# A list scheduler's model of VectorE and GpSimd: mutual exclusion in place of a share, and ScalarE's table loads counted

## The chip, the cores and the metric

The kernel runs on one core of a Trainium2 chip, as one program. The metric is device time in microseconds (us): the median of several executions. Engines are called by their names: TensorE (PE in the profile, its weight loads PEld), VectorE (DVE), ScalarE (ACT), GpSimd (POOL) and SyncE (SP). SP and GpSimd also issue the transfers (DMAs) of this kernel.

## The reference

The kernel computes a small encoder in float32: one batch of 512 tokens with 1024 features, two layers. Each layer has four sub-steps, and every one adds its result to the input and normalises:

```python
for i in range(DEPTH):
    y = swiglu(x, ffn_w_gate[i, 0], ffn_w_up[i, 0], ffn_w_down[i, 0])
    x = layer_norm(ALPHA * x + 0.5 * y, ln_g[i, 0], ln_b[i, 0])
    y = mixer_ab(...) if i % 2 == 0 else mixer_c(...)
    x = layer_norm(ALPHA * x + y, ln_g[i, 1], ln_b[i, 1])
    y = memory_attn(x, mem, mem_w_q[i], mem_w_kv[i], mem_w_o[i])
    x = layer_norm(ALPHA * x + y, ln_g[i, 2], ln_b[i, 2])
    y = swiglu(x, ffn_w_gate[i, 1], ffn_w_up[i, 1], ffn_w_down[i, 1])
    x = layer_norm(ALPHA * x + 0.5 * y, ln_g[i, 3], ln_b[i, 3])
```

`swiglu` is silu(x W_gate) * (x W_up) W_down with 2816 hidden features. `mixer_ab` has eight dense attention heads (A, with RMS-normed queries and keys) and eight heads in a window of 128 tokens to either side with a sink (B); both get rotary positions. `mixer_c` is a neighbourhood attention of 16 heads on an 8 by 64 grid with a learned bias. `memory_attn` attends to 256 memory tokens with four heads.

## The kernel before

**Tiling and stages.** Every float32 operand of a matmul is split into a high and a low part (`split`): ScalarE rounds it to the fast float32 format, VectorE subtracts the rounded value from the original, and a product is three matmuls (`mm3`). The split subtractions, 128 partitions by 1024 or 512 columns, are the bulk of VectorE's work. The eight stages run one after the other with some overlap: feed-forward, mixer AB, memory attention, feed-forward, feed-forward, mixer C, memory attention, feed-forward. The feed-forward parts save multiplications with seven products for eight (`quarters`, `down_steps`), whose sums VectorE makes, in part with DMAs that add (issued by GpSimd).

**What GpSimd computes.** It multiplies softmax weights by the reciprocal of their sums (`normalise`, form t<-t,l; some go to VectorE as a tensor_scalar), adds the two halves of the rotary embedding (`rope`, form slab<-t,t), subtracts the bias from the mask in mixer C (t<-near,t), adds collected sums to the rows (`gather`, form x<-x,slab), and takes the reciprocal square roots of the norms (`rsqrt`, tiles lny, rms2y, rms8y). Beside that it issues DMAs. In the feed-forward parts it does hardly anything but issue DMAs; in the mixers it computes all the time.

**The scheduler.** The kernel isn't issued as it is written. A `Graph` records every instruction of every engine as an `Op` with an estimate of its duration (`cost`, lines 113 to 134; for VectorE 72 ns and columns/0.96, halved columns for a tensor_scalar in SBUF, 60 ns for each per-row scalar; for GpSimd 2.4 ns a column and 70 ns when both operands are dense, else 1.7 and 130), its dependencies and the tiles it holds. `emit` (from line 290) then calls `plan` twice. `plan` (from line 175) is a simulation of a list schedule: for each engine it keeps the operations whose operands have landed, takes the engine that can start first, gives it the operation of the smallest key, and sets its stop and the time its result lands. Tiles come free in the plan when their last user has landed, and go to waiting tiles in the order of the program. In the first pass the key is the place in the program. Between the passes `deadlines` works out for every operation the latest start, back from TensorE's due times. In the second pass that is the key for VectorE, ScalarE and GpSimd; TensorE and SyncE keep the program's order among what is ready. The order in which the second plan starts the operations is the order in which they are issued, engine by engine. On the chip each engine follows its list in order and waits on semaphores for real results. So the plan's times decide orders alone: an operation that the plan thinks early can sit at the head of its engine's list and wait.

**What the plan knew of VectorE and GpSimd together.** `record` marks an operation as `plain` if it is a tensor_tensor without a PSUM operand. When a plain operation of VectorE is planned, 35% of the time that it overlaps with the last four plain operations of GpSimd is added to it. GpSimd's own operations are never made longer, and no other kind of operation is. Loads of ScalarE's function table aren't planned at all.

**Names in the profile.** All instructions recorded have one line, L150 (`op.call`), so groups are told apart by tile: slab, raw and t are tiles in SBUF; a, d and t as the output of a matmul are PSUM banks (t takes mostly transposes; t also names SBUF tiles of 512 columns); x are the rows, xh and xl their split transposes.

Of the kernel before, what the change touches and what calls it, by code (L numbers as in the profile page):

```python
# [16 lines left out]
AF = mybir.ActivationFunctionType  # L17
# [22 lines left out]

class Op:
    __slots__ = (
        "engine", "adds", "ns", "call", "deps", "users", "wait", "ready", "end", "frees", "index", "rank", "dma", "size", "plain",
        "key", "start", "stop", "lands", "later",
    )

# [19 lines left out]
class Graph:  # L66
# [69 lines left out]
    def record(self, engine, method, args, kw):  # L136
        kw = dict(kw)
        aps = [z for z in list(args) + list(kw.values()) if hasattr(z, "tensor")]
        outs = [kw[k] for k in ("out", "accum_out") if k in kw]
        if "out" not in kw:  # L140
            outs.insert(0, args[0])
        ins = [z for z in aps if not any(z is o for o in outs)]
        op = Op()
        op.engine, op.index, op.dma, op.adds = engine, len(self.ops), method == "dma_start", "accum_op" in kw
        op.rank = op.index
        op.ns = self.cost(engine, method, outs[0], ins, kw)
        op.size = math.prod(outs[0].shape) * 4
        op.plain = method == "tensor_tensor" and all(z.space != bass.MemoryType.PSUM for z in ins + outs)
        fn = getattr(getattr(self.nc, engine), method)
        op.call = lambda: fn(*args, **kw)  # L150
        op.deps, op.users, op.frees, op.later = set(), [], [], []
        if self.after and engine in self.after[1]:
            op.deps.add(self.after[0])
        for z, writes in [(z, False) for z in ins] + [(z, True) for z in outs]:
            info = self.tiles.get(z.tensor.name)
            if info is None:
                continue
            p0, p1, runs = self.extent(z)
            opens = writes and kw.get("start", False)
            keep = []  # L160
            for q, w, a0, a1, other in info["log"]:
                over = opens or p0 < a1 and a0 < p1 and (
                    info["bank"] and q.engine != engine or any(l < b and a < h for l, h in runs for a, b in other)
                )
                if over and (w or writes or info["bank"] and q.engine != engine) and q is not op:
                    op.deps.add(q)
                covered = writes and p0 <= a0 and a1 <= p1 and all(any(l <= a and b <= h for l, h in runs) for a, b in other)
                if not covered:
                    keep.append((q, w, a0, a1, other))
            keep.append((op, writes, p0, p1, runs))  # L170
            info["log"] = keep
            info["users"].add(op)
        self.ops.append(op)

    def plan(self):

        for info in self.tiles.values():
            info["left"], info["at"], info["behind"] = len(info["users"]), 0.0, None
        now = {e: 0.0 for e in self.ENGINES}
        heaps = {e: [] for e in self.ENGINES}  # L180
        ready = {e: [] for e in self.ENGINES}
        free = {s: [(0.0, i, None) for i in range(s.bufs)] for s in self.spaces.values()}
        turn = {s: 0 for s in free}
        queues = {True: [(0.0, 0.0)], False: [(0.0, 0.0)]}
        busy, order = [], []
        for op in self.ops:
            op.wait, op.ready = len(op.deps) + len(op.frees), 0.0

        def release(op, t):
            op.ready = max(op.ready, t)  # L190
            op.wait -= 1
            if op.wait == 0:
                heapq.heappush(heaps[op.engine], (op.ready, op.key, op.index, op))

        def grant(space):

            while turn[space] < len(space.queue) and free[space]:
                info = space.queue[turn[space]]
                turn[space] += 1
                if info["users"]:  # L200
                    t, _, info["behind"] = heapq.heappop(free[space])
                    for op in info["users"]:
                        release(op, t)

        def arrive(e):
            while heaps[e] and heaps[e][0][0] <= now[e]:
                _, key, i, op = heapq.heappop(heaps[e])
                heapq.heappush(ready[e], (key, i, op))

        for op in self.ops:  # L210
            if op.wait == 0:
                heapq.heappush(heaps[op.engine], (0.0, op.key, op.index, op))
        for space in free:
            grant(space)
        while len(order) < len(self.ops):
            best = None
            for e in self.ENGINES:
                arrive(e)
                if ready[e] and e in self.PATIENT:
                    key, _, op = ready[e][0]  # L220
                    for at, k, _, _ in heapq.nsmallest(4, heaps[e]):
                        if at < now[e] + op.ns * 0.6 and k < key - self.margin:
                            now[e] = at
                            arrive(e)
                            break
                if ready[e]:
                    t = now[e]
                elif heaps[e]:
                    t = heaps[e][0][0]
                else:  # L230
                    continue
                if best is None or t < best[0]:
                    best = (t, e)
            assert best, "no instruction can start"
            t, e = best
            if not ready[e]:
                now[e] = t
                continue
            _, _, op = heapq.heappop(ready[e])
            shared = lambda pairs, a, b: sum(max(0.0, min(b, y) - max(a, x)) for x, y in pairs)  # L240
            stop = t + op.ns
            if op.plain and e == "vector":
                stop += 0.35 * shared(busy[-4:], t, stop)
            elif op.plain and e == "gpsimd":
                busy.append((t, stop))
            lands = stop + self.LATENCY[e]
            if op.dma:
                kind = e == "sync"
                work = op.size / 2**19 * (4000.0 if op.adds else 1650.0)
                begin = max(stop + (1200.0 if kind else 2000.0), queues[kind][-1][1])  # L250
                finish = begin + work + 0.5 * shared(queues[not kind][-6:], begin, begin + work)
                queues[kind].append((begin, finish))
                lands = finish + 790.0
            op.start, op.stop, op.lands, now[e] = t, stop, lands, stop
            order.append(op)
            for u in op.users:
                release(u, stop if e == u.engine == "tensor" else lands)
            for info in op.frees:
                info["left"] -= 1
                info["at"] = max(info["at"], lands)  # L260
                if info["left"] == 0:
                    heapq.heappush(free[info["space"]], (info["at"], len(order), info))
                    grant(info["space"])
        return order
# [1364 lines left out]
```

## Time and profile before

| what | us |
|---|---|
| median of 3 runs | 2147.38 (2145.44 to 2148.2) |
| the profiled execution's own time | 2146.44 |
| its span, first to last instruction | 2144.3 |
| TensorE busy | 2117.4 |
| VectorE busy | 1761.6 |
| ScalarE busy | 1082.3 |
| GpSimd busy | 377.2 |

The span is what the trace sees of the profiled execution; that execution's own time is 2.1 us more. Groups in the profile read: line, engine, operation, output<-inputs, shape, count, then busy time in all, mean duration of one in ns, and idle time of the engine just before them with what ended it. In views of waits the columns after the names are the total, how often, and the longest. In the windows view each engine's busy time is followed by its number of instructions in brackets, and after GpSimd come the granted clock of TensorE, the busy share of the DMA engines and GB/s. TensorE's matmuls overlap and their ends are modelled, so its busy time is not proof of full speed. The timeline's rows are start, length, engine, operation and count, with idle time before it in square brackets.

The stages in this trace, by the tiles that they touch: feed-forward to about 315 us, mixer AB to 580, memory attention to 770, two feed-forward parts to 1400, mixer C to 1620, memory attention to 1840, feed-forward to 2115, and the last norms and stores to 2144.

### The profile page before, as it was taken

What the parts mean: (1) busy time and instruction counts of PE and PEld (TensorE: products, weight loads), DVE (VectorE), ACT (ScalarE), POOL (GpSimd) and SP (SyncE); (2) the same over time, 40 slices, a digit from 0 to 9 for tenths busy, and PEclk for the clock granted to TensorE, in tenths of its full rate; (3) what the DMA queues carried; (4) which work ended last, traced back from release to release, by engine and by line L of the source; (5) the groups of instructions that cost most, each with busy time, mean ns of one, the idle gap of its engine ahead of it and who ended that gap; (6) DMA issues with size and microseconds to landing.
All of it is one profiled execution on the core that took longest, in us unless ns stands there. A gap on an engine that the chain in (4) does not pass through costs nothing.

```text
span 2144.3 us, 33147 instructions
## 1 busy us (share of the span) xinstructions
PE 2117.4 (99%) x12904; PEld 1884.7 (88%) x12904; DVE 1761.6 (82%) x2501; ACT 1082.3 (50%) x1703; POOL 377.2 (18%) x483
## 2 busy tenths in 40 slices
PE   9999999999999999999999999999999999999997
PEld 7999988778888899999889999888888888999996
DVE  7789988898748869999879999876677478699996
ACT  5555543576435545455545455445554355444552
POOL 0001114544002000000200000413420021000003
PEclk9999999999999999999999999999999999999999
DMA  6566562003443246665445556455454432456551
GB/s 201 141 167 147 139 184 86 20 20 83 145 146 99 89 108 187 158 147 139 128 108 126 141 137 179 111 139 143 134 152 157 137 100 89 109 148 155 140 148 59
DMA packets 208716, 275.95 MB, mean 129 GB/s; under 512 B 10672, under 2 KB 151600, under 8 KB 208560
## 3 DMA queue, kind: packets, MB, share of 16 engines
q1 hardware_dynamic: 175760, 221.14, 33.1%
q0 software_dynamic: 32512, 52.44, 13.8%
q8 instruction: 102, 1.67, 0.3%
q14 instruction: 54, 0.44, 0.1%
q10 hardware_dynamic: 288, 0.26, 0.0%
HBM read 259.12 MB, written 4.19 MB: 123 GB/s over the span
## 4 chain that ended last, share of the span: by engine, by line
PE 87%; DVE 7%; ACT 2%; POOL 2%; issue 1%; DMA 1%; SPq 0%; POOLq 0%; DVEq 0%; ACTq 0%
PE a L150 55%; PE d L150 19%; PE t L150 13%; DVE slab L150 4%; DVE x L150 1%; DVE t L150 1%; ACT t L150 1%; ACT slab L150 1%; POOL slab L150 1%; POOL x L150 0%; DVE mn L150 0%; DVE xl L150 0%; DMA raw<-x_t 0%; POOL rms8y L150 0%; SPq L150 0%
## 5 line engine op out<-in xcount | busy, mean ns | idle before, releaser
L150 DVE TENSOR_TENSOR slab<-slab,slab 128x1024 fp32r<-128x1024 f32 (+3 forms) x638 | 726.5, 1164 | 73.1 <-ACT slab L150 35.3
L150 ACT CAST slab<-slab 128x1024 fp32r<-128x1024 f32 (+2 forms) x498 | 472.6, 983 | 342.3 <-DVE slab L150 140.1
L150 PE MATMUL a<-slab,slab 128*128 128x256 f32 (+2 forms) x2456 | 566.2, 314 | 1.7 <-DVE slab L150 1.1
L150 PE MATMUL a<-xh,slab 128*128 128x256 f32 (+2 forms) x2480 | 560.4, 315 | 0.3
L150 PE MATMUL d<-slab,slab 128*128 128x512 f32 (+2 forms) x1856 | 448.8, 382 | 0.6 <-DVE x L150 0.4
L150 PEld LDWEIGHTS a<-slab,slab 128*128 128x128 f32 x2456 | 416.8, 190 | 34.7 <-DVE slab L150 2.4
L150 PEld LDWEIGHTS a<-xh,slab 128*128 128x128 f32 x2480 | 416.7, 191 | 34.1 <-ACT slab L150 1.1
L150 PE MATMUL a<-xl,slab 128*128 128x256 f32 (+1 forms) x1240 | 390.2, 315 | 0.0
L150 PE MATMUL a<-raw,slab 128*128 128x256 f32 x2048 | 388.7, 283 | 0.0
L150 PEld LDWEIGHTS d<-slab,slab 128*128 128x128 f32 x1856 | 328.3, 189 | 58.5 <-DVE x L150 2.5
L150 PEld LDWEIGHTS a<-raw,slab 128*128 128x128 f32 x2048 | 327.8, 192 | 5.1 <-ACT slab L150 0.3
L150 PEld LDWEIGHTS a<-xl,slab 128*128 128x128 f32 x1240 | 236.4, 191 | 18.3 <-DVE xl L150 0.4
L150 PE MATMUL t<-slab,slab 128*128 128x512 f32 (+1 forms) x864 | 210.6, 384 | 1.0 <-DVE x L150 1.0
L150 DVE TENSOR_TENSOR slab<-raw,slab 128x1024 fp32r<-128x1024 f32 (+2 forms) x132 | 167.8, 1285 | 22.2 <-ACT slab L150 22.1
L150 PEld LDWEIGHTS t<-slab,slab 128*128 128x128 f32 x864 | 151.1, 189 | 27.5 <-issue 1.9
L150 ACT CAST slab<-t 128x512 fp32r<-128x512 f32 (+2 forms) x211 | 114.2, 565 | 79.7 <-PE t L150 47.5
L150 ACT CAST slab<-raw 128x1024 fp32r<-128x1024 f32 (+1 forms) x124 | 123.6, 1021 | 39.1 <-DMA raw<-mem_w_kv 8.7
L150 DVE TENSOR_TENSOR slab<-t,slab 128x512 fp32r<-128x512 f32 (+2 forms) x211 | 131.5, 642 | 11.9 <-ACT slab L150 10.8
L150 POOL TENSOR_TENSOR t<-t,l 128x256 f32<-128x256 f32 (+2 forms) x104 | 86.3, 852 | 282.0 <-DVE l L150 281.8
L150 DVE SCALAR_TENSOR_TENSOR x<-d,x 128x512 f32<-128x512 f32 x168 | 114.7, 684 | 16.7 <-PE d L150 16.5
L150 ACT COPY t<-a 128x512 f32<-128x512 f32 x96 | 56.4, 588 | 126.0 <-PE a L150 73.1
L150 POOL DMA_DIRECT2D slab<-ffn_w_down x40 | 47.8, 1194 | 317.0 <-DVE slab L150 303.4
(127 smaller groups left out, 2171.5 us busy)
## 6 DMA issues: line engine op xcount, KB each, us to landing
slab<-ffn_w_gate SPq DMA_DIRECT2D x80, 512.0 KB
slab<-ffn_w_up SPq DMA_DIRECT2D x80, 512.0 KB
slab<-ffn_w_down SPq DMA_DIRECT2D x80, 512.0 KB
slab<-ffn_w_down POOLq DMA_DIRECT2D x40, 512.0 KB, 5.6
raw<-mem_w_kv SPq DMA_DIRECT2D x16, 1024.0 KB
slab<-t SPq DMA_DIRECT2D x96, 128.0 KB
slab<-ffn_w_gate POOLq DMA_DIRECT2D x16, 512.0 KB, 7.7
slab<-ffn_w_up POOLq DMA_DIRECT2D x16, 512.0 KB, 5.8
```

The lines of the kernel that those rows point to most:

```text
L150: op.call = lambda: fn(*args, **kw)
```

## The change

`record` now marks as `port` every tensor_tensor, scalar_tensor_tensor and tensor_scalar of GpSimd, and those of VectorE whose planned time is over 250 ns and whose inputs are all in SBUF. When such an operation is planned, it is made longer by the whole time that the other engine's last such operation still has to run, and its own stop is what the other engine's next one has to wait for. This works both ways, and the share is gone. `record` also keeps the function of a ScalarE activation if it is Silu or Exp; where it differs from the one planned before, 1290 ns are added. The estimates of `cost`, the tiles, the deadlines' rule and the instructions themselves are the same.

```diff
@@ -144,8 +144,12 @@
         op.engine, op.index, op.dma, op.adds = engine, len(self.ops), method == "dma_start", "accum_op" in kw
         op.rank = op.index
         op.ns = self.cost(engine, method, outs[0], ins, kw)
+        func = args[2] if method == "activation" else None
+        op.table = str(func) if func in (AF.Silu, AF.Exp) else None
         op.size = math.prod(outs[0].shape) * 4
-        op.plain = method == "tensor_tensor" and all(z.space != bass.MemoryType.PSUM for z in ins + outs)
+        op.port = method in ("tensor_tensor", "scalar_tensor_tensor", "tensor_scalar") and (
+            engine == "gpsimd" or engine == "vector" and op.ns > 250.0 and all(z.space != bass.MemoryType.PSUM for z in ins)
+        )
         fn = getattr(getattr(self.nc, engine), method)
         op.call = lambda: fn(*args, **kw)
         op.deps, op.users, op.frees, op.later = set(), [], [], []
@@ -182,7 +186,7 @@
         free = {s: [(0.0, i, None) for i in range(s.bufs)] for s in self.spaces.values()}
         turn = {s: 0 for s in free}
         queues = {True: [(0.0, 0.0)], False: [(0.0, 0.0)]}
-        busy, order = [], []
+        held, order, table = [0.0, 0.0], [], None
         for op in self.ops:
             op.wait, op.ready = len(op.deps) + len(op.frees), 0.0
 
@@ -239,10 +243,12 @@
             _, _, op = heapq.heappop(ready[e])
             shared = lambda pairs, a, b: sum(max(0.0, min(b, y) - max(a, x)) for x, y in pairs)
             stop = t + op.ns
-            if op.plain and e == "vector":
-                stop += 0.35 * shared(busy[-4:], t, stop)
-            elif op.plain and e == "gpsimd":
-                busy.append((t, stop))
+            if op.port:
+                stop += max(0.0, held[e == "vector"] - t)
+                held[e != "vector"] = stop
+            if op.table and op.table != table:
+                stop += 1290.0
+                table = op.table
             lands = stop + self.LATENCY[e]
             if op.dma:
                 kind = e == "sync"
```

The slot names of `Op` follow (`port` and `table` in place of `plain`).

More of the change, by code (lines that the diff above doesn't have):

```diff
@@ L42 @@
     __slots__ = (
-        "engine", "adds", "ns", "call", "deps", "users", "wait", "ready", "end", "frees", "index", "rank", "dma", "size", "plain",
+        "engine", "adds", "ns", "call", "deps", "users", "wait", "ready", "end", "frees", "index", "rank", "dma", "size", "port", "table",
         "key", "start", "stop", "lands", "later",
```

## The prediction

> **What bounds the kernel now.** I read the page first: how busy each engine is over the span.
>
> ```profile
> span 2144.3 us, 33147 instructions
> PE 2117.4 (99%) x12904; PEld 1884.7 (88%) x12904; DVE 1761.6 (82%) x2501; ACT 1082.3 (50%) x1703; POOL 377.2 (18%) x483
> PE 87%; DVE 7%; ACT 2%; POOL 2%; issue 1%; DMA 1%; SPq 0%; POOLq 0%; DVEq 0%; ACTq 0%
> ```
>
> TensorE is busy for 2117.4 us of 2144.3, and the chain that ended last is 87% TensorE. The change removes no instruction and adds none, it only writes the same ones in another order. So all that it can win are the 26.9 us in which TensorE stands idle, and what it can lose is more such time. The second view is the windows view by stage, with TensorE's busy time as the second column after the length, then the weight loads, VectorE, ScalarE and GpSimd.
>
> ```profile
> 0.00:30.00 30.00, 28.57 (x112) 21.15 (x113) 22.94 (x28) 20.77 (x28) 0.73 (x7) 1.00 0.90 298
> 30.00:315.00 285.00, 285.00 (x1886) 262.55 (x1885) 246.34 (x284) 146.43 (x187) 27.07 (x24) 1.00 0.59 148
> 315.00:580.00 265.00, 255.78 (x1354) 213.15 (x1353) 227.75 (x479) 146.84 (x317) 115.56 (x160) 1.00 0.24 71
> 580.00:770.00 190.00, 189.08 (x1022) 162.54 (x1021) 129.62 (x182) 88.34 (x148) 25.65 (x28) 1.00 0.37 111
> 1400.00:1620.00 220.00, 217.98 (x1377) 194.09 (x1375) 155.20 (x332) 114.48 (x259) 67.19 (x122) 1.00 0.52 148
> 1620.00:1840.00 220.00, 219.08 (x1193) 188.83 (x1192) 154.67 (x218) 104.94 (x174) 26.70 (x33) 1.00 0.37 115
> 1840.00:2115.00 275.00, 274.77 (x1841) 253.93 (x1840) 243.51 (x285) 136.44 (x172) 29.88 (x25) 1.00 0.52 134
> 2115.00:2144.30 29.30, 17.67 (x78) 14.07 (x76) 20.08 (x35) 4.97 (x8) 8.25 (x9) 0.87 0.24 72
> ```
>
> The idle time by stage is length less busy: 1.4 us at the start, nothing in the first feed-forward part (30 to 315), **9.2 us in mixer AB** (315 to 580), 0.9 in the first memory attention, 2.0 in mixer C (1400 to 1620), 0.9 in the second memory attention, 0.2 in the last feed-forward part, and 11.6 in the tail (the half us that is left lies in the feed-forward parts between), where the last rows are normalised and written. The granted clock stands at 1.00 in every stage but the tail, so the clock is no part of it. In mixer AB VectorE is busy for 227.75 of 265 us and GpSimd for 115.56, its longest use anywhere: that is where a rule on the two of them must bite.
>
> The third view is the waits of TensorE in that stage.
>
> ```profile
> PE t L150 <- DVE slab L150: 3.2, 5, 0.9
> PE t L150 <- POOL slab L150: 2.8, 4, 1.1
> PE a L150 <- DVE slab L150: 1.1, 2, 0.8
> PE t L150 <- DVE x L150: 0.8, 1, 0.8
> ```
>
> All four are waits for a result of VectorE or GpSimd, and three of them stand before work in bank t, which in this stage is nearly all transposes. These four lines hold 7.9 of the 9.2 us.
>
> **Does the trace show the exclusion that the change assumes?** I compare like instructions with GpSimd at work and without.
>
> ```profile
> L150 DVE TENSOR_TENSOR slab<-slab,slab 128x1024 f32<-128x1024 f32 x140 | 170.7, 1220 | 10.5 <-PE t L150 6.6 <-DMA slab<-ffn_w_down 1.6 <-DMA slab<-ffn_w_up 0.6
> L150 DVE TENSOR_TENSOR slab<-raw,slab 128x1024 fp32r<-128x1024 f32 x15 | 21.0, 1417 | 0.0
> L150 DVE TENSOR_SCALAR t<-t,l 128x512 f32<-128x512 f32 x8 | 8.2, 1028 | 0.1
> L150 DVE SCALAR_TENSOR_TENSOR x<-d,x 128x512 f32<-128x512 f32 x168 | 114.7, 684 | 16.7 <-PE d L150 16.5
> L150 POOL TENSOR_TENSOR slab<-t,t 128x512 f32<-128x512 f32 x4 | 6.0, 1510 | 7.4 <-DVE t L150 7.4
> L150 POOL TENSOR_TENSOR x<-x,slab 128x512 f32<-128x512 f32 x36 | 57.9, 1631 | 10.3 <-DVE x L150 5.8 <-DVE slab L150 3.9
> ```
>
> A 128x1024 subtraction of two SBUF tensors takes 1220 ns on average over the kernel and 1417 in mixer AB. Normalising 512 columns takes VectorE 1028 ns, though the planner's formula gives it 399 (512/2/0.96 + 72 + 60, lines 122 to 126), and the old rule adds nothing to it, since it is no tensor_tensor. GpSimd's adds of 512 columns take 1510 and 1631 where its formula gives 1299 (2.4 for an element and 70), and the old plan never delays GpSimd. The form with one operand in PSUM (x<-d,x) stays at 684. So the forms that the change names are those that the rows show stretched, and it lets the others alone.
>
> The timeline of one stall shows the mechanism, first VectorE, then GpSimd, then TensorE:
>
> ```profile
> 374.55 0.28 DVE L150 TENSOR_REDUCE rh<-t 128x2 f32<-128x128 f32 x1
> 374.75 2.09 DVE L150 TENSOR_TENSOR slab<-raw,slab 128x1024 fp32r<-128x1024 f32 x1
> 373.57 2.18 POOL L150 TENSOR_TENSOR slab<-t,t 128x512 f32<-128x512 f32 x1 [2.20 <-DVE t L150]
> 375.81 0.33 PE L150 MATMUL t<-ident,slab 128*128 128x128 f32 x1 [1.06 <-POOL slab L150]
> ```
>
> The rotary add on GpSimd, issued at 373.57, took 2.18 us because VectorE was in a subtraction of two SBUF tensors; the next subtraction then took 2.09 us in place of 1.22, since GpSimd was still in its add. TensorE's next transpose had been put behind that add and waited 1.06 us. A planner that had known of it would have put other matmuls there. Mixer C has one more (VectorE's subtraction 1.54 us beside GpSimd's bias sums):
>
> ```profile
> 1441.24 1.54 DVE L150 TENSOR_TENSOR slab<-raw,slab 128x1024 fp32r<-128x1024 f32 x1
> 1443.44 0.66 PE L150 MATMUL t<-ident,t 128*128 128x128 f32 x4 [0.83 <-DVE t L150]
> ```
>
> and the two memory attentions one each, on a subtraction of 2.26 us, for 0.21 us:
>
> ```profile
> 692.29 2.26 DVE L150 TENSOR_TENSOR slab<-raw,slab 128x1024 fp32r<-128x1024 f32 x1
> 695.21 0.50 PE L150 MATMUL d<-slab,slab 128*128 128x512 f32 x1 [0.21 <-DVE x L150]
> ```
>
> **The change part by part.** It removes the 35% share of overlap for plain tensor_tensor operations, adds mutual exclusion with the full rest of the other's time, and adds 1290 ns where ScalarE goes between Silu and Exp. None of it is an instruction, a semaphore or a transfer: what changes is the order on TensorE (lowest rank that the plan thinks ready), on VectorE, ScalarE and GpSimd (latest permissible start, from the first plan), and the order of DMA issues in SP's and GpSimd's queues, which follows the same planned times. Waits that the hardware makes stay exactly as they are for a given order.
>
> *The feed-forward parts.* Apart from GpSimd's adds at their ends its instructions there are DMA issues, which the new rule does not name, and TensorE was busy for 285.00 of 285.00 us. I cost it at nothing. The cover is TensorE's backlog; an order that broke it would show there first.
>
> *Waits behind a stretched operation.* 1.06 in AB, 0.83 in C, twice 0.21 in the memory attentions: 2.3 us. A plan that knows the stretch puts other ready matmuls in the hole. I take all of it, minus 2.3; the other bound is nothing.
>
> *The rest of mixer AB's waits.* 9.2 less 1.06 is 8.2 us. They stand behind operations that were not stretched themselves, but the plan around them was early: by the rows above it is short by 8 x (1028 - 399) = 5.0 us for the normalising and by 15 x (1417 - 1220) = 3.0 us, less the share it added, for the subtractions. About 8 us of missing VectorE time in a stage with 9.2 us of waits is of the right size, but a plan that is right only in the mean still leaves single waits. I take half, minus 4.1, with bounds of 0 and minus 8.2.
>
> *The rest in C and the memory attentions.* 2.0 + 0.9 + 0.9 less the 1.25 above is 2.6 us. VectorE has room there (155.20 of 220), so neither a gain nor a loss is plain. I take 0, bounds minus 2.6 and plus 2.6.
>
> *The table loads.*
>
> ```profile
> L150 ACT ACT_TABLE_LOAD x6 | 7.7, 1283 | 2.6 <-PEq L1622 1.7 <-DVE mn L150 0.9
> 1433.95 0.60 ACT L150 ACTIVATE t<-d 128x512 fp32r<-128x512 f32 x1 [3.70 <-PE d L150]
> 1434.57 1.28 ACT L150 ACT_TABLE_LOAD   x1
> 1435.86 0.46 ACT L150 ACTIVATE t<-t,mn 128x192 f32<-128x192 f32 x1
> ```
>
> Six loads of 1283 ns in the whole kernel, 1290 in the plan, and none that another order saves, for the stages follow each other. ScalarE is 50% busy. I cost it at 0, between plus and minus 1.3 (one load exposed or covered).
> The Trainium skill, page "ScalarE: Activation LUTs", section "What ACT_TABLE_LOAD costs", adds to the load a drain of about 1380 ns at every switch. By that the plan would still be short by 1.4 us at each switch, and the stages' first heads would come late as before. The trace disagrees: the next activation starts 1.29 us after the load did, and the load came 0.02 us behind the activation before it.
>
> *The tail.*
>
> ```profile
> 2135.47 1.00 POOL L150 TENSOR_SCALAR lny<-var 128x1 f32<-128x1 f32 x1 [3.30 <-ACT junk L150]
> 2136.55 1.47 POOL L150 TENSOR_TENSOR lny<-lny,nhalf 128x1 f32<-128x1 f32 x1
> 2138.05 1.41 DVE L150 SCALAR_TENSOR_TENSOR x<-slab,lny,slab 128x512 f32<-128x512 f32 x2 [0.44 <-POOL lny L150]
> L150 POOL TENSOR_TENSOR lny<-lny,nhalf 128x1 f32<-128x1 f32 x32 | 19.6, 614 | 2.7
> L150 POOL TENSOR_SCALAR lny<-var 128x1 f32<-128x1 f32 x32 | 11.2, 350 | 184.6 <-ACT junk L150 184.5
> ```
>
> The last two GpSimd steps took 2.47 us against a mean of 0.96: VectorE was in steps that read two SBUF tensors. The new plan sees this, but its choice is still "whatever is ready first", and VectorE has nothing else ready. I take 0, with minus 1.5 if it gets out of the way and plus 1.3 (one 128x1024 step more in front).
>
> **Sum:** -2.3 - 4.1 = -6.4 us. The profiled execution took 2146.44 us, 2.1 more than its span, and comes to 2140.0; the median of the runs shown is 0.9 above it, so on the median's scale 2147.4 - 6.4 = **2141.0 us**. With every bound on the good side it is 2147.4 - 2.3 - 8.2 - 2.6 - 1.3 - 1.5 = 2131.5, but all five at once is hardly likely, and I set the low end at 2133.
>
> **The rivals.** *The waits only move.* VectorE and GpSimd have the same work to do in mixer AB, and the exclusion takes its toll in any order; the new plan counts it but never chooses whom to let go first. Then TensorE waits elsewhere for as long, and the time is 2147 within 4 us. For it: VectorE's 227.75 of 265 us. Against it: TensorE has other matmuls in this stage (projections, output shares) that a better informed order can put in the holes. The Trainium skill, page "SBUF — State Buffer", section "Who interferes with whom", says that the one who issues first gets the pair for the whole instruction and the other blocks in full, and its summary advises to give way to the critical one. By that rule, counting alone wins nothing. The timeline at 373 to 376 agrees on the blocking. This way also takes in that the order hardly changes at all. Chance 0.2.
>
> *Slower: the fill is spent too early.* TensorE's order in the plan takes the lowest rank that is ready. If the plan holds the softmax chain back, projections and shares that now cover mixer AB's windowed heads move ahead of them, and the last heads are left bare. It decides where the plan's delay of a head exceeds one piece of fill. If each of the eight windowed heads then meets one more wait of the size of mixer C's 0.83 us, that is 6.6 us: 2154.0. For it: the plan now charges VectorE for every small GpSimd step also where none would collide on the chip, and each such charge pulls fill forward. Against it: a plan that is too late fills holes that do not come, which costs nothing by itself. Chance 0.35.
>
> **How the numbers follow.** The forecast has 0.45, the standing still 0.2, the loss 0.35. About 0.2% (4.3 us) is what a measurement of this kernel can tell from no change; the forecast's 6.4 lies beyond it, so faster 0.45, same 0.2, slower 0.35. The range reaches from 2133 to the slower rival with the tail's 1.3 us on top, 2155. The likeliest case's own range is 2133 to 2143.
>
> **What would show it.** In the profile after: TensorE's idle time in 315 to 580 falls from 9.2 to about 4 to 5 us; the waits "PE t <- POOL slab" and "PE t <- DVE slab" shrink; 30 to 315 stays full. VectorE's and GpSimd's stretched forms should keep about their means (1417, 1028, 1510), for the gain is in what TensorE does meanwhile. I am wrong if mixer AB's idle time stays or grows, if a feed-forward part shows idle time, or if the difference lies in the tail.

## The result and the profile after

The changed kernel takes 2139.8 us (median of 7 runs, 2137.6 to 2140.7) against 2146.8 us (7 runs, 2145.4 to 2148.2): a ratio of **0.9966, with a 95% interval of 0.9954 to 0.9977**, so 7.1 us are gone (4.9 to 9.9 by the interval). The forecast was 2141.0 us. The profiled execution took 2138.68 us.

The page of the changed kernel, its span, its engines and its chain:

```profile
span 2136.9 us, 33147 instructions
PE 2114.8 (99%) x12904; PEld 1885.1 (88%) x12904; DVE 1764.7 (83%) x2501; ACT 1081.7 (51%) x1703; POOL 379.9 (18%) x483
PE 95%; DVE 3%; ACT 1%; issue 1%; DMA 0%; POOL 0%; POOLq 0%; DVEq 0%; SPq 0%; ACTq 0%
```

The work is the same to the instruction. TensorE's idle time fell from 26.9 to 22.1 us, by 4.8, while the span fell by 7.4. At least a part of the other 2.6 us is again waiting: a matmul of 512 columns is drawn 0.39 us long where the next one starts 0.23 us after it, so a wait is longer than the idle time drawn for it. The chain that ended last is 95% TensorE in place of 87%: it passes less often through VectorE (3% after 7%) and GpSimd (0% after 2%). The windows view of the changed kernel, with the same columns as before:

```profile
315.00:580.00 265.00, 259.53 (x1384) 217.21 (x1383) 232.12 (x482) 148.96 (x319) 117.00 (x160) 1.00 0.24 75
580.00:770.00 190.00, 189.54 (x1027) 163.34 (x1026) 132.05 (x183) 89.96 (x151) 26.68 (x29) 1.00 0.37 111
1400.00:1620.00 220.00, 219.81 (x1380) 196.26 (x1380) 155.61 (x332) 115.91 (x260) 66.47 (x122) 1.00 0.54 156
1620.00:1840.00 220.00, 219.55 (x1214) 190.46 (x1213) 156.48 (x217) 105.51 (x174) 28.21 (x33) 1.00 0.38 114
```

Idle in mixer AB: 5.5 us (9.2 before). In mixer C 0.2 (2.0), in the memory attentions 0.5 each (0.9 each). The stages end a little earlier in this trace, so fixed windows blur them. I therefore also add up, for each kernel, the usual distance between starts of every matmul (227 ns for 512 columns, 174 for 384, 120 for 256, 91 for 192; a transpose is set at 70), and compare at what time two traces have done the same sum. This "offset at equal work" says where time was won, to some tenths of a microsecond. It is worked out from the starts of all 12,904 matmuls of each trace, and the headings name the time in the trace of before:

| kernel | 306 us | 416 | 585 | 766 | 1042 | 1396 | 1611 | 1843 | 2120 |
|---|---|---|---|---|---|---|---|---|---|
| changed | -0.3 | -5.0 | -3.6 | -4.5 | -5.0 | -5.5 | -6.4 | -7.2 | -7.7 |
| excl_only | -0.2 | -4.7 | -4.9 | -5.1 | -5.6 | -5.7 | -4.7 | -4.8 | -5.3 |
| table_only | -0.4 | -2.6 | -2.4 | -3.2 | -3.2 | -3.2 | -3.9 | -4.8 | -4.8 |
| pe_new | -0.3 | +0.4 | +0.5 | 0.0 | 0.0 | +1.2 | +0.8 | +0.2 | +0.2 |
| pe_old | +0.1 | -0.1 | +3.4 | +2.7 | +2.5 | +8.5 | +9.8 | +10.1 | +9.6 |
| pool_waits | -0.6 | -3.6 | -3.4 | -2.8 | -2.8 | -2.8 | -2.2 | -1.8 | -1.8 |
| dve_waits | +0.4 | -2.5 | -3.0 | -3.4 | -3.9 | -4.3 | -4.4 | -4.8 | -5.3 |
| dve_waits_table | +0.4 | -3.5 | -3.9 | -5.2 | -5.7 | -6.1 | -7.6 | -8.9 | -9.4 |

Each row is one execution, the profiled one. For pe_old that was the slowest of six (2156.0 us, median 2153.2), so its row overstates the loss.

In the changed kernel 4.7 us are won between 306 and 416, where mixer AB's projections and first heads run; 1.4 are given back by 585. Then 0.9 are won in the first memory attention (585 to 766), 0.9 in mixer C (1396 to 1611), 0.8 in the second memory attention (1611 to 1843), and 0.5 in each of three later stretches of feed-forward work.

The waits of TensorE in mixer AB after the change, to be held against those of before:

```profile
PE t L154 <- DVE slab L154: 2.6, 4, 1.5
PE d L154 <- DVE x L154: 1.0, 2, 0.6
PE a L154 <- ACT t L154: 0.5, 1, 0.5
```

The 2.8 us behind GpSimd's rotary adds are gone altogether. Here is the place of the quoted stall, first VectorE, then GpSimd, then TensorE:

```profile
373.39 1.89 DVE L154 TENSOR_TENSOR slab<-raw,slab 128x1024 fp32r<-128x1024 f32 x1
376.40 1.22 DVE L154 TENSOR_TENSOR slab<-raw,slab 128x1024 fp32r<-128x1024 f32 x1
372.91 1.29 POOL L154 TENSOR_TENSOR slab<-t,t 128x512 f32<-128x512 f32 x1 [1.49 <-DVE t L154]
374.90 0.27 PE L154 MATMUL t<-ident,slab 128*128 128x128 f32 x1
```

The rotary add now starts before the subtraction and takes 1.29 us in place of 2.18. The subtraction pays instead (1.89), and the second one has moved behind to 376.40. TensorE's transpose has nothing to wait for. So it was not TensorE's list alone that changed, VectorE's did too. The groups of mixer AB, in the same window as before, show the shift:

```profile
L154 POOL TENSOR_TENSOR slab<-t,t 128x512 f32<-128x512 f32 x4 | 5.2, 1292 | 8.9 <-DVE t L154 8.9
L154 DVE TENSOR_SCALAR t<-t,l 128x512 f32<-128x512 f32 x8 | 10.5, 1312 | 0.0
L154 DVE TENSOR_TENSOR slab<-raw,slab 128x1024 fp32r<-128x1024 f32 x16 | 22.0, 1393 | 0.0
```

GpSimd's adds of 512 columns went from a mean of 1510 to 1292 ns, VectorE's normalising from 1028 to 1312. Each mean hangs on one instruction: of the four adds only the one at 373 us had been stretched, and one of the eight normalisings now takes 2.68 us. GpSimd's 16 adds of 256 columns went the other way, from a mean of 743 to 850 ns. Over the whole kernel VectorE is busy for 1764.7 us after 1761.6, GpSimd for 379.9 after 377.2; share_030 below, with nearly the lists of before, differs from before by as much on VectorE (1758.8). So the toll didn't visibly shrink, it moved to other instructions.

The 1.4 us given back have their main part at 426 us:

```profile
417.75 1.04 POOL L154 TENSOR_TENSOR t<-t,l 128x512 f32<-128x512 f32 x1 [0.36 <-DVE l L154]
418.73 1.85 POOL L154 MEMSET slab<- 128x1024 f32 x2
418.17 2.68 DVE L154 TENSOR_SCALAR t<-t,l 128x512 f32<-128x512 f32 x1
424.60 1.26 DVE L154 TENSOR_SCALAR t<-t,l 128x512 f32<-128x512 f32 x1
425.78 0.68 DVE L154 TENSOR_TENSOR slab<-t,slab 128x512 fp32r<-128x512 f32 x1
426.51 0.66 PE L154 MATMUL t<-ident,t 128*128 128x128 f32 x4 [1.48 <-DVE slab L154]
```

The normalising at 424.60, beside three of GpSimd's, is no worse than in before, where one took 1.27 us at 426.26. The lateness comes from the one at 418.17: it took 2.68 us, where 0.49 is the shortest of its form. It began beside a normalising of GpSimd, and ended only 0.27 us after the two memsets that followed there. From there to the subtraction at 425.78 VectorE was never idle, so the 2.2 us were passed on, and the transpose behind that subtraction waited 1.48 us. In excl_only (below) the same normalising takes 0.47 us, ahead of the memsets, and the wait at this place isn't there. So the new wait is for the most part one that the plan didn't know of: the new rule names three forms of GpSimd's, and memset isn't one of them.

### The profile page after: what moved, and what is told of

Its sections match the earlier page's. It is cut to its first block, busy times and chain, and to the rows that moved or that the text cites. A ratio compares the mean times of both kernels' runs of the same rounds, so it can differ in the third digit from the quotient of the medians.

```text
span 2136.9 us, 33147 instructions
## 1 busy us (share of the span) xinstructions
PE 2114.8 (99%) x12904; PEld 1885.1 (88%) x12904; DVE 1764.7 (83%) x2501; ACT 1081.7 (51%) x1703; POOL 379.9 (18%) x483
## 4 chain that ended last, share of the span: by engine, by line
PE 95%; DVE 3%; ACT 1%; issue 1%; DMA 0%; POOL 0%; POOLq 0%; DVEq 0%; SPq 0%; ACTq 0%
PE a L154 58%; PE d L154 22%; PE t L154 15%; DVE slab L154 1%; DVE x L154 1%; ACT slab L154 1%; DVE t L154 0%; ACT t L154 0%; DMA slab<-t 0%; DMA raw<-x_t 0%; DVE mn L154 0%; POOL t L154 0%; DVE xl L154 0%; POOLq L1631 0%; ACT xh L154 0%
```

## The experiments

My theory was that of the prediction: the exclusion makes the plan true in mixer AB, and TensorE's order gains by it. The rivals were that the table loads do it, that the other engines' orders do it, and that any reshuffle would have moved the time as much. Every kernel was run against the kernel before on the same chip. Each kernel changes the planning alone, and all compute the same.

**excl_only** takes the three lines on `table` out of the changed kernel.

```diff
-            if op.table and op.table != table:
-                stop += 1290.0
-                table = op.table
```

> The exclusion without the charge for ScalarE's table loads. If the exclusion brings the gain (my theory): nearly all of it, 2138 to 2142 us against about 2147 before, with the idle time of TensorE in mixer AB near the 5.5 us of the changed kernel. If the table loads bring it: 2145 to 2148 us.

Measured: 2141.8 us, ratio 0.9976 (0.9967 to 0.9986). Within what the theory expected. By the medians it is 1.8 us short of the changed kernel's gain, but the two intervals overlap. Where it falls short is seen in the windows. Mixer AB's idle time is even lower, 4.2 us; mixer C and the second memory attention win nothing:

```profile
315.00:580.00 265.00, 260.77 (x1394) 218.49 (x1393) 229.60 (x483) 150.01 (x321) 117.67 (x160) 1.00 0.25 75
1400.00:1620.00 220.00, 218.20 (x1371) 194.46 (x1371) 153.94 (x329) 116.12 (x260) 65.42 (x121) 1.00 0.54 154
1620.00:1840.00 220.00, 219.09 (x1201) 189.42 (x1200) 155.50 (x216) 103.64 (x172) 27.98 (x33) 1.00 0.38 113
```

The stall that the prediction quoted from mixer C is still there, on the same subtraction beside the same bias sums, and has grown from 0.83 to 1.49 us:

```profile
1437.08 1.54 DVE L154 TENSOR_TENSOR slab<-raw,slab 128x1024 fp32r<-128x1024 f32 x1
1439.27 1.25 PE L154 MATMUL t<-ident,t 128*128 128x128 f32 x8 [1.49 <-DVE t L154]
```

The two waits of 0.21 us in the memory attentions have grown to 0.40. In table_only, the next run, TensorE doesn't wait at that place of mixer C at all. So in mixer C and the memory attentions it is not the exclusion that removes the waits.

**table_only** keeps the old share and takes only those three lines (with `op.table`) from the change.

```diff
+            if op.table and op.table != table:
+                stop += 1290.0
+                table = op.table
```

> The old share of 0.35 kept, and only the table loads counted. My theory: 2145 to 2148 us, no gain. Rival (the table loads put the first heads of each attention right): 2139 to 2142 us.

Measured: 2141.7 us, ratio 0.9976 (0.9966 to 0.9985). My theory missed, the rival came true: the table loads alone win as much as the exclusion alone. It is won at four places, read off the offset at equal work: 2.2 us at 386 to 416, 0.8 at the end of the first memory attention, 1.1 at the start of mixer C, 0.9 at the end of the second. The first is where ScalarE goes over to Exp. In the timeline of before:

```profile
394.18 1.28 ACT L150 ACT_TABLE_LOAD   x1 [0.91 <-DVE mn L150]
395.47 0.69 ACT L150 ACTIVATE t<-a,mn 128x512 f32<-128x512 f32 x1
396.15 0.54 ACT L150 ACTIVATE slab<-t 64x128 fp32r<-64x128 f32 x2
396.73 0.61 DVE L150 SCALAR_TENSOR_TENSOR slab<-t,slab 64x128 fp32r<-64x128 f32 x2 [1.44 <-ACT slab L150]
397.06 0.73 PE L150 MATMUL a<-slab,slab 128*128 128x512 f32 x2 [0.77 <-DVE slab L150]
```

The load pushes the Exp back, the Exp pushes back the scaling of a query block (slab<-t) that stands behind it in ScalarE's list, VectorE waits 1.44 us for that, and TensorE's scores wait 0.77 us for VectorE. With the load counted, in the timeline of table_only, the scores stand later in TensorE's list:

```profile
396.43 0.55 ACT L155 ACTIVATE slab<-t 64x128 fp32r<-64x128 f32 x2
397.57 0.39 PE L155 MATMUL d<-slab,xh 128*128 128x512 f32 x1
397.80 1.07 PE L155 MATMUL a<-slab,slab 128*128 128x512 f32 x4
```

The scaling is no earlier, 2.6 us after the load began in place of 2.0, but projections (d<-slab,xh and xl) run in the meantime, and the scores wait for nothing. The second place is 19 us behind a load of Silu's table, at the gated products of the next feed-forward part. In before:

```profile
742.73 3.49 DVE L150 TENSOR_TENSOR slab<-slab,slab 128x1024 f32<-128x1024 f32 x3
746.14 0.41 DVE L150 TENSOR_TENSOR t<-d,t 128x256 f32<-128x256 f32 x1
746.60 0.44 PE L150 MATMUL t<-ident,t 128*128 128x128 f32 x2 [0.59 <-DVE t L150]
```

and in table_only:

```profile
739.86 3.49 DVE L155 TENSOR_TENSOR slab<-slab,slab 128x1024 f32<-128x1024 f32 x3
743.27 0.42 DVE L155 TENSOR_TENSOR t<-d,t 128x256 f32<-128x256 f32 x1
743.91 0.38 PE L155 MATMUL t<-ident,t 128*128 128x128 f32 x2
```

Three sums of 1024 columns stand in front of the product that TensorE's transpose waits for. Now they come 2.9 us earlier; 2.4 of these are the lead that the whole trace has by then, so against TensorE's work it is 0.5. TensorE's list has five matmuls in front of that transpose in place of three, and it waits for nothing. The last of the four places is like it, a wait of 0.59 us at 1820, 19 us behind the other load of Silu's table. In excl_only both waits are still there, with 0.48 us. That a load reaches so far through the planned times is what the one edit shows; by which step, I didn't follow.

**share_030 and share_040** are reshuffles without a reason, in the kernel before; share_040 has 0.40 there.

```diff
-                stop += 0.35 * shared(busy[-4:], t, stop)
+                stop += 0.30 * shared(busy[-4:], t, stop)
```

> A shuffle without a reason: the kernel before with a share of 0.30 in place of 0.35. It moves some 20 lines of TensorE's list. If only a truer plan wins: within 3 us of the time before. Rival (any reordering of this size moves the time by some 5 us, and counting table loads was luck): 4 us or more to either side.

> A second shuffle: a share of 0.40, some 70 lines of TensorE's list, more than the table loads alone moved (45). The same expectations: within 3 us of the time before if only a truer plan wins, 4 us or more to either side if chance does it.

Measured: 2146.6 us, ratio 1.0004 (0.9995 to 1.0012), and 2145.7 us, ratio 0.9996 (0.9987 to 1.0005). Neither differs from before. So a reordering of this size isn't worth 5 us by itself. Counted in the planned lists, table_only has another instruction than before at 85 places of TensorE's list, share_040 at 89, share_030 at 34. On VectorE's list, though, it is 73 places against 24 and 13, so the shuffles are milder there. That the 5 us are luck is less likely by these two runs, not excluded. The places speak more plainly. Of the twelve kernels that were planned by one rule throughout, the five that count the loads (changed, table_only, dve_waits_table, table_2660, calibrated) have none of the three waits at 746, 1443 and 1820 us of before. The seven that don't count them, both shuffles among them, have all three, of 0.5 to 1.5 us.

**pe_new and pe_old** ask which engine's list carries the gain. Both rules are in the kernel; the first double pass of planning uses one, its order for TensorE is kept, and a second double pass with the other rule must follow that order on TensorE. For pe_new:

```diff
+        for self.new in (True, False):
...
+            if pinned:
+                for i, op in enumerate(pinned):
+                    op.key = i
             order = self.plan()
+            self.pinned = [op for op in order if op.engine == "tensor"]
```

with `plan` starting on TensorE only the next of `self.pinned`; pe_old has the two rules the other way round.

> TensorE's order is that of the changed kernel, instruction by instruction; the other engines' orders are planned by the old rule around it. My theory (the gain lies in what TensorE does while VectorE and GpSimd hold each other up): most of the gain stays, 2139 to 2143 us. Rival (the orders on VectorE, GpSimd and ScalarE carry it): 2145 to 2148 us.

> The counterpart: TensorE's order is that of the kernel before, the others are planned by the new rule around it. My theory: little or nothing is won, 2144 to 2149 us. Rival (the other engines' orders carry the gain): 2139 to 2142 us.

Measured: pe_new 2147.5 us, ratio 1.0002 (0.9993 to 1.0011); pe_old 2153.2 us, ratio 1.0028 (1.0016 to 1.0040). In pe_new my theory missed and the rival's range was met; in pe_old both missed, so the rival falls too. TensorE's new order with the others planned by the old rule wins nothing; orders planned by the new rule around TensorE's old one cost 6 us. In pe_new the first heads come too late for TensorE:

```profile
410.17 2.04 POOL L155 TENSOR_TENSOR t<-t,l 128x512 f32<-128x512 f32 x2 [4.85 <-DVE l L155]
411.26 0.44 PE L155 MATMUL t<-ident,t 128*128 128x128 f32 x2 [1.28 <-POOL t L155]
```

In pe_old the largest wait lies between two feed-forward parts, where neither kernel has one:

```profile
1070.81 2.35 DVE L155 TENSOR_TENSOR slab<-slab,slab 128x1024 fp32r<-128x1024 f32 x2
1072.09 0.51 PE L155 MATMUL a<-slab,xh 128*128 128x512 f32 x1 [1.92 <-DVE slab L155]
```

TensorE's list doesn't carry the gain by itself, and neither do the others' without it: here the lists had to come from one and the same plan. The new list of VectorE, ScalarE or GpSimd alone was not tried.

**pool_waits and dve_waits** take the exclusion one way, without the table loads. For dve_waits:

```diff
-                stop += max(0.0, held[e == "vector"] - t)
+                stop += max(0.0, held[1] - t) * (e == "vector")
```

pool_waits has `held[0]` and "gpsimd" there.

> The exclusion one way, without the table loads: GpSimd's operations are lengthened by VectorE's, not VectorE's by GpSimd's. In the stall at 373 us GpSimd's rotary add was the late one. Theory A (the plan was early on GpSimd's rotary adds, and that made the stalls between 375 and 395 us): those two waits go, minus 2 us or more there, 2142 to 2145 us in all. Theory B (VectorE's missing time is what counts): they stay, 2146 to 2148 us.

> The other way alone: VectorE's operations are lengthened by GpSimd's, not GpSimd's by VectorE's, no table loads. Theory A: the waits between 375 and 395 us stay, 2145 to 2148 us. Theory B: they go, and the time is 2141 to 2144 us. If both are needed together, neither of the two runs comes near the 2141.8 us of the two-way exclusion.

Measured: pool_waits 2144.9 us, ratio 0.9994 (0.9985 to 1.0003), no difference shown; dve_waits 2140.6 us, ratio 0.9974 (0.9963 to 0.9984), as much as both ways together (2141.8). In places theory A had it right: with dve_waits the stall at 374 us stays, if shorter (0.62 us), and with pool_waits that at 374 shrinks (0.17). By 416 us the two are alike: pool_waits has won 3.0 us there, dve_waits 2.9, the exclusion both ways 4.5. But pool_waits gives 1.8 of it back by the end, and dve_waits adds small sums at many later places, so over the kernel theory A was wrong: pool_waits lies in its range, dve_waits lies below the ranges of both theories. That VectorE's time is charged at all is the larger half.

**share_10** charges VectorE's tensor_tensor with the whole overlap, by the old code (1.0 in place of 0.35).

> The old rule with a share of 1.0: VectorE's tensor_tensor alone is lengthened, by the whole overlap with GpSimd's tensor_tensor; no other forms, no table loads. If the amount of time charged to VectorE is what wins: 2140 to 2143 us, like the one-way exclusion. If the forms left out (tensor_scalar, scalar_tensor_tensor) matter: 2144 to 2147 us.

Measured: 2144.5 us, ratio 0.9991 (0.9982 to 1.0000). By the medians 1.8 us, a third of what dve_waits wins, and at the edge of what can be told. The wait in full, and the forms that the old rule left out (tensor_scalar, scalar_tensor_tensor), matter beside the size of the share; the run doesn't part these two.

**table_2660** is the changed kernel with 2660.0 for 1290.0.

> The changed kernel with 2660 ns charged for a table load, which is the load with the drain that the Trainium skill adds to it. If the 1283 ns of the trace are the whole price, a plan that is 1.4 us too late at each switch is no better and perhaps worse than the changed kernel: 2139 to 2144 us. If the drain were real: 2135 to 2138 us.

Measured: 2139.9 us, ratio 0.9971 (0.9960 to 0.9982). No better than 1290 and not clearly worse. A charge of twice the size does as well, within the noise, so the exact size of the charge isn't what wins.

**dve_waits_table** has dve_waits' line in the changed kernel, so the table loads are counted.

> Only VectorE's operations are lengthened by GpSimd's (the half that won 5.7 us alone), and the table loads are counted. If the two gains add up, as they lie in different places (table loads at 397 to 409, 746, 1442 and 1820 us; the one-way exclusion spread over mixer AB and the ends of the feed-forward parts): 2136 to 2139 us, better than the changed kernel. If they meet in the same stalls, as in the changed kernel: 2139 to 2142 us.

Measured: 2137.2 us, ratio **0.9959 (0.9947 to 0.9972)**, the lowest of all. By the medians the parts add up to 11.1 us (5.4 of table_only and 5.7 of dve_waits), and 9.1 are there, spread as the offsets show. That is in the range expected for gains that add up. Its windows:

```profile
315.00:580.00 265.00, 259.86 (x1389) 217.81 (x1388) 228.56 (x481) 149.64 (x319) 115.26 (x160) 1.00 0.25 74
580.00:770.00 190.00, 189.97 (x1028) 163.67 (x1027) 132.40 (x185) 90.71 (x152) 26.82 (x29) 1.00 0.38 113
1620.00:1840.00 220.00, 219.97 (x1214) 190.75 (x1213) 155.38 (x217) 106.79 (x176) 28.31 (x33) 1.00 0.38 115
```

Both memory attentions are full. Against the changed kernel the median is 2.6 us lower, but the two intervals overlap: that it beats it isn't shown.

**calibrated** gives GpSimd's operations, in the changed kernel, their undisturbed durations.

```diff
-        return n * (2.4 if dense else 1.7) + (70 if dense else 130)
+        return n * (2.1 if dense else 1.65) + (205 if dense else 193)
```

> The changed kernel with GpSimd's own costs set to the undisturbed durations of the trace (1.65 ns a column and 193 ns with a broadcast operand, 2.1 and 205 ns with two dense ones, in place of 1.7 and 130, 2.4 and 70). If a truer plan wins in proportion: 1 to 4 us below the changed kernel, 2136 to 2139 us. If what is left to win is beyond the plan's grain: within 2 us of it, or above.

Measured: 2138.8 us, ratio 0.9965 (0.9953 to 0.9978). 1 us below the changed kernel and within its interval: nothing can be told.

## Why the prediction came out right, and where it didn't

**The sum was right, its parts weren't.** Forecast -6.4 us, measured -7.1 us, by order alone, as said. That the two lie so close is luck in good part: a term put at nothing wins as much alone as the two terms that I counted.

- *The feed-forward parts at nothing*: right in their bodies, where the offset at equal work stands still for 250 us at a time. At 129 us TensorE waited once, 0.9 us, and the start had been 1.3 us earlier; share_030, whose lists are those of before at that place, shows the same (1.6 us earlier, then a wait of 1.18), so it belongs to the execution and not to the change. At three ends the waits beside `gather`, of 0.2 us of idle time, are gone, worth 0.5 each by the offset, which I hadn't counted. They go with the exclusion: excl_only has none of them, table_only all three.
- *Waits behind a stretched operation, -2.3*: 1.06 in AB and 0.83 in C are gone, the two of 0.21 in the memory attentions are not, they doubled to 0.4. And of those gone only the 1.06 goes with the exclusion. With the exclusion alone the wait in C grows to 1.49, with the table loads alone it is gone: I put the 0.83 down to the wrong part of the change.
- *Half of the rest of mixer AB, -4.1*: with the 1.06 that made -5.2 for the stage; the idle time fell by 3.7, and the offset by 3.3. Too much by 1.5 to 1.9, which is the size of the new wait of 1.48 us. The exclusion alone, without that wait, has 4.2 us of idle time left there, a fall of 5.0. So in mixer AB the step was sized about right.
- *The rest in C and the memory attentions at 0, within 2.6*: C and the two memory attentions lost 2.8 us of idle time in all (1.8, 0.5 and 0.5), of which 0.83 in C was counted in the step of the stretched operations. That leaves 1.9: my bound held, the value didn't. The exclusion alone takes no more than 0.3 us of idle time out of the three.
- ***The table loads at 0, within 1.3***: **this step failed.** Alone they win 5.4 us (0.15 to 0.34% by the interval). I priced the load as an instruction: ScalarE has half its time free, no order saves a load. But the load was there before and after. What the plan lacked was its lateness, 1.28 us at the head of a chain that goes through ScalarE, VectorE and TensorE, and with it operations behind it were listed too early on three engines, as the timeline at 394 us shows. The right question is who was listed on the strength of the missing time.
- The sum came out because the exclusion alone wins 5.3 us, about what I gave to its two steps (6.4), and because the two parts together make 7.1 and not 10.7. They overlap at 386 to 416 us: with the exclusion alone no wait is left there, so the 2.2 us of the table loads at that place can't be won a second time. And the changed kernel has the wait of 1.48 us at 426, which neither part has alone.

**"The gain is in what TensorE does meanwhile" fell.** pe_new has precisely TensorE's new list and wins nothing. And the stretched forms didn't keep their means: of the three that I named, GpSimd's adds of 512 columns got quicker (1510 to 1292) and VectorE's normalising slower (1028 to 1312); the subtraction stayed (1417 and 1393). The row of 1220 ns that I held against the 1417 is one of the feed-forward sums and not of a split subtraction. The price is the same, though: the subtraction at 376.40 in the changed kernel took 1.22 us.

**The rivals.** "The waits only move" had it half right, for VectorE's and GpSimd's toll did move and not shrink, but TensorE waits less for it: 5.5 us of idle time in mixer AB after 9.2. The Trainium skill's rule ("SBUF — State Buffer", "Who interferes with whom") that the first to issue holds the pair is what the timeline shows at 373 us in both kernels, once with GpSimd as the loser, once with VectorE. That counting alone would win nothing, which I had drawn from it, doesn't hold: a plan that counts also shifts who issues first. "The fill is spent too early" didn't come about: the lead over the kernel before was 3.4 us at 440 and 3.6 at 585, so the windowed heads cost nothing more. The table loads weren't among my rivals, and should have been.

**The tail** took 12 us as before: its last GpSimd steps are stretched still.

**On the drain.** The Trainium skill ("ScalarE: Activation LUTs", "What ACT_TABLE_LOAD costs") adds about 1380 ns to a load. Here the Exp starts 1.29 us after the load began, at 394.18 and 395.47: no drain appears there. The run with 2660 ns doesn't contradict this, nor could it have shown it alone.

**What stays open.** Why the one-way exclusion with the table loads does at least as well as the two-way one (the wait of 1.48 us at 426, which it doesn't have, is a part of it); by what steps a load reaches a wait 19 us on; whether any other delay charged to ScalarE at these places would do the same; and how large chance is at the first place, 386 to 416 us, for two idle shuffles are a thin measure of it.

## What to carry to other kernels

When an order is made by a plan, price a cost that the plan lacks by what stands behind it in every engine's list, not by whether the engine that pays it has time to spare: here table loads of 1.3 us each on an engine that is half idle were worth 5 us in all. A better estimate need not remove the delay to win, it is enough that the list has other work in front of the one that waits. Take all lists from the same plan: here half a new order was worth nothing or less. When a rule on two engines goes into a plan, look for the forms that it doesn't name: here two memsets fit the larger part of the 1.4 us given back. Before crediting a gain of a quarter of a per cent to a mechanism, take the parts one by one, and run a shuffle that means nothing.

## What the runs showed of the hardware that I had not expected

- A scalar_tensor_tensor on VectorE that reads two SBUF tensors holds up even GpSimd's smallest steps. In the tail of the changed kernel the last two steps on one column a partition took 1.00 and 1.47 us, as before:

```profile
2127.75 1.00 POOL L154 TENSOR_SCALAR lny<-var 128x1 f32<-128x1 f32 x1 [3.31 <-ACT junk L154]
2128.83 1.47 POOL L154 TENSOR_TENSOR lny<-lny,nhalf 128x1 f32<-128x1 f32 x1
2128.61 1.28 DVE L154 SCALAR_TENSOR_TENSOR x<-slab,lny,slab 128x1024 f32<-128x1024 f32 x1
```

The root, at 2128.83, ended 0.4 us after VectorE's step that began at 2128.61 did. Over the kernel before the two steps had means of 350 and 614 ns and took 0.18 and 0.55 us at the least. In every run of this case the last root took 1.47 us: some 1.5 us at the very end of the program, with the step before it, that the orders hardly touched.

- Two memsets of GpSimd, 128x1024 each, met a tensor_scalar of VectorE over 512 columns once, at 418 us in the changed kernel (shown above): it ended after both and took 2.68 us, where 0.49 is the shortest of its form. Scalar_tensor_tensors that read two SBUF tensors met the same memsets in the trace of before (at 337 and 345 us, 128x1024) and took 1.28 us, the mean of their form over the kernel. So here the memset held up the one form and not the other; the first is a single case.
